# Where the Fourier groups put their second output half, and when the attention's score blocks are transposed, in a two-layer encoder kernel

## The chip, the cores and the metric

The kernel runs on one core of a Trainium2 chip. Its five instruction streams are TensorE (PE: matmuls, with its weight loads shown as PEld), VectorE (DVE), ScalarE (ACT), GpSimd (POOL) and SyncE (SP, which only issues transfers here). Each executes its own instructions in the order in which they stand in the program and waits at semaphores for the others. The metric is the device time of the core in microseconds, the median of several runs. Lower is better.

## The reference

Two encoder layers work on 272 tokens (16 learned ones ahead of 256) of width 2048, all in float32. Cut to what matters:

```python
for i in range(DEPTH):
    proj = rmsnorm(h_stream) @ w_in[i]            # q | k | v | f | gate a | gate f
    q, k = rope(rmsnorm(q, q_norm)), rope(rmsnorm(k, k_norm))
    s = einsum('bqkgd,bskd->bkgqs', q, k) / sqrt(HEAD_DIM)
    attn = einsum('bkgqs,bskd->bqkgd', softmax(s), v)           # 8 heads, 2 key/value heads
    fr = fft2(f.reshape(B, L, 8, 128), axes=(1, 3), norm="ortho").real
    merged = sigmoid(ga) * (attn @ w_attn_br[i]) + sigmoid(gf) * (fr @ w_four[i])
    h_stream += merged @ w_out[i]
    up = rmsnorm(h_stream) @ w_up[i]
    h_stream += (silu(dwconv3(up_gate)) * up_val) @ w_down[i]
return h_stream[:, N_META:]
```

## The kernel before

**Matmuls and weights.** Each operand is split into a high and a low part, and each product is three matmuls (high by high, high by low, low by high). Weights arrive as chunks of 128 x 1024 values (512 KB), in one fixed order over the whole kernel, by SP into five buffers `raw`. ACT copies each to its high part `wh` (line 303) and DVE subtracts to get the low part `wl` (line 306). There are four buffers of each, so that the splitting runs up to four chunks ahead of TensorE. A chunk of a plain group feeds 24 matmuls of 272 columns.

**Groups.** `group` (line 349 on) computes 256 output channels by 272 tokens: two chunks deep for the branch outputs `a` (attention) and the output projection `o`, four chunks for the gates `ga` and `gf`. It takes two PSUM banks. `four_group` (line 391 on) does the same for the Fourier branch `s`, in another form: its two halves m=0 and m=1 of 128 channels each take two banks (even and odd parts), are one chunk and 17 matmuls each, and are evacuated one after the other by `s_evac` (from line 1204): ACT copies `se` and `so` out (line 1207), DVE adds the other halves of the banks to them (line 1208), combines them (1210, 1211) and multiplies by the gate (1213). `s_evac` is given one buffer each of `se` and `so`, so that ACT's copy for m=1 follows DVE's line 1211 for m=0. In layer 0 the `s` chunks are first folded by DVE (line 291).

**PSUM.** There are eight banks: four under the tag "mm", which the groups take in turn, and four under "aux", which the small products take: norm statistics, score blocks `ps_s` (lines 1070 to 1072), their transposes `ps_pt` (line 1094), values `ps_pv` (lines 1117 to 1120), sums of squares `ps_ss` (line 920). The Fourier banks are also called `ps_s` in the profile; lines 409, 410 and 415 tell them apart from the scores.

**Small products between the big ones.** They are generators. After every second pair of channel tile and half (6 matmuls of a plain group, some 0.7 us) the helper `step` lets one of them go on; a `yield n` waits for n such steps. `drain` runs all of them to their end at once, with nothing between; it is called ahead of the first `a` group of a layer. So the order is that of the program text, and then a scheduler shifts instructions a little on each engine.

**Attention.** For each of the two key/value heads nine score blocks are computed: one for the learned tokens of four heads, then two blocks of 128 queries for each of four heads. A round of the loop at line 1126 issues one block's scores, takes its maximum (DVE, 1074 and 1076), its exponential with the row's sum (ACT, 1080 and 1081), two steps later the reciprocal of that sum (DVE, 1086) and the scaling of the block (POOL, 1087), and one step later the three transposes of the block *before* (PE, 1094), which ACT and DVE split into `PH` and `PL` (1107, 1108, 1110). Values of a head follow a round after its second block was transposed. Three buffers `pn` hold the exponentials. The attention of a layer starts under the `q` and `ga` groups and runs under `ga` and `gf`.

**q's norm.** `q_stage` (line 1013) gets the sums of squares of q by transposes and a reduction, makes mean plus epsilon of them (line 1030), raises that to the power -0.5 on POOL (line 515), and `attention` multiplies the result by 1/sqrt(128) (line 1049). The result scales the scores inside the exponential.

**Order of the branches.** After the `q` groups come, in the first half, `ga0 ga1 ga2 ga3 gf0 gf1 s0 gf2 a0 s1 gf3 a1 s2 ga4 a2 s3 gf4 a3`, then eight `o` groups; in the second half `s4 a4 ga5 gf5 s5 a5 ga6 gf6 s6 a6 ga7 gf7 s7 a7`, then eight `o` groups. So each layer has eight `s` groups, and each is followed at once by another group.

Of the kernel before, what the change touches and what calls it, by code (L numbers as in the profile page):

```python
# [10 lines left out]
F32 = mybir.dt.float32  # L11
# [167 lines left out]
def encoder_kernel(ctx, tc, xT, params, consts, bmat, cfold, csign, w_fl, w_f64c, w_in, w_abr, w_four, w_f64, w_out, w_up, w_down, w_vn, w_dn, w_dt, out):  # L179
# [211 lines left out]
    def four_group(key, fr, x64, w64, evac):  # L391
        k, chs = order[st["grp"]]
        assert k == key, (k, key)
        st["grp"] += 1
        i0 = st["next"]
        st["next"] += len(chs)
        advance(i0 + 1 + LOOK)
        for m in range(MG):
            sl = slice(m * P, (m + 1) * P)
            ps = [psum.tile([P, 512], F32, tag="mm", name=f"ps_s{m}{e}") for e in range(2)]  # L400
            pump(i0 + m)
            h, lo = (w.rearrange("p c n -> p (c n)").rearrange("p (e k n) -> p e k n", e=2, k=4) for w in splits.pop(i0 + m))
            for j in range(2):
                for c in range(2):
                    kt = 2 * j + c
                    for e in range(2):
                        x = al(fr[:, kt, e])
                        o2 = st2(ps[e][:, :2 * TH].rearrange("p (r n) -> p r n", r=2))
                        nc.tensor.matmul(o2, h[:, e, kt], x, start=kt == 0, stop=False)
                        nc.tensor.matmul(st2(ps[e][:, :TH]), lo[:, e, kt], x[:, 0], start=False, stop=e == 1 and kt == 3)  # L410
                    step()
                    pump()
                if m == 0 and j == 1:
                    advance(i0 + 2 + LOOK)
            nc.tensor.matmul(st2(ps[0][:, :TH]), w64[:, sl], al(x64), start=False, stop=True)
            evac(m, ps)
# [194 lines left out]
    for l in range(DEPTH):  # L611
# [6 lines left out]
        with tc.tile_pool(name=f"mix{l}", bufs=1) as mp:  # L618
# [386 lines left out]
            push(vtrans(), 4)  # L1005

            qvs, qsms, rqs = [], [], []
            pns = [mp.tile([P, 3 * P], F32, name=f"pn{i}") for i in range(3)]
            cnt = [0]
            for pn in pns:  # L1010
                nc.gpsimd.memset(pn[:, 0:P], 0.0)
# [1 line left out]
            def q_stage(i, qp, qsq, qs):  # L1013
                kv, j = i // 2, i % 2
                sl = slice(2 * j, 2 * j + 2)
                if j == 0:
                    qvs.append(small.tile([P, 9], F32, tag="qv", name="qv"))
                    qsms.append(small.tile([P, 2, 4, NM], F32, tag="sqm", name="sqm", bufs=2))
                qv, qsm = qvs[kv], qsms[kv]
                yield 3  # L1020
                nc.vector.tensor_copy(qsm[:, :, 2 * j:2 * j + 2, :], qsq[:, :, 0:NM].unsqueeze(1).to_broadcast([P, 2, 2, NM]))
                d4 = qv[:, 4 * j:4 * j + 4]
                sums_t(d4, [qsq[:, m, a:b] for m in range(MG) for a, b in BLK[1:]])
                d4 = d4.rearrange("p (m i) -> p m i", m=2)
                nc.vector.tensor_tensor(d4, d4, bc2(tok2[:, 1:3]), op=ALU.mult)
                if j:
                    yield 1
                    sums_t(qv[:, 8:9], [qsm.rearrange("p r h t -> p (r h t)")])
                    nc.vector.tensor_tensor(qv[:, 8:9], qv[:, 8:9], tok2[:, 0:1], op=ALU.mult)
                    nc.vector.tensor_scalar(qv, qv, 1.0 / HD, EPS, op0=ALU.mult, op1=ALU.add)  # L1030
                    rq = small.tile([P, 9], F32, tag="rq", name="rq")
                    pow_half(rq, qv)
                yield 6 - j
                yield from rope(qp, qs, qH[kv][:, sl, :], qL[kv][:, sl, :])
                if j:
                    rqs.append(rq)
                    if kv == 0:
                        push(attend(), 5)
# [7 lines left out]
                    yield from attention(kv, rqs[kv])  # L1046

            def attention(kv, rq):
                nc.vector.tensor_scalar(rq, rq, 1.0 / math.sqrt(HD), None, op0=ALU.mult)
                qm = mp.tile([P, 2, 2, 4, NM], F32R, tag="qm", name="qm")  # L1050
                for j, src in enumerate((qH, qL)):
                    nc.scalar.copy(qm[:, j], src[kv][:, :, 0:NM].bitcast(F32).unsqueeze(1).to_broadcast([P, 2, 4, NM]))
# [7 lines left out]
                def scores(item):  # L1060
                    if item is None:
                        lh, ll, rcol = qmh, qml, rq[:, 8:9]
                    else:
                        h, i = item
                        c0, c1 = BLK[1 + i]
                        lh, ll = qH[kv][:, h, c0:c1], qL[kv][:, h, c0:c1]
                        rcol = rq[:, 2 * h + i:2 * h + i + 1]
                    ss = psum.tile([P, 512], F32, tag="aux", name="ps_s")
                    so = st2(ss[:, :T])
                    nc.tensor.matmul(so, lh, al(kH[:, kv, :]), start=True, stop=False)  # L1070
                    nc.tensor.matmul(so, lh, al(kL[:, kv, :]), start=False, stop=False)
                    nc.tensor.matmul(so, ll, al(kH[:, kv, :]), start=False, stop=True)
                    mx = small.tile([P, 1], F32, tag="mx", name="mx")
                    nc.vector.tensor_reduce(mx, ss[:, :T], axis=AX.X, op=ALU.max)
                    nb = small.tile([P, 1], F32, tag="nb", name="nb")
                    nc.vector.tensor_scalar(nb, mx, rcol, -1.0, op0=ALU.mult, op1=ALU.mult)
                    pn = pns[cnt[0] % 3]
                    cnt[0] += 1
                    sm = small.tile([P, 1], F32, tag="sm", name="sm")
                    nc.scalar.activation(hv(pn[:, P - NM:3 * P]), de(ss[:, :T]), AF.Exp, bias=nb, scale=rcol, accum_out=sm)  # L1080
                    nc.scalar.copy(pn[:, 0:96].rearrange("p (a b) -> p a b", b=32)[:, :, 0:NM], _rep(pn[:, P - NM:P], 3))
                    return pn, sm
# [39 lines left out]
                    nc.vector.tensor_tensor(hv(qL[kv][:, h, lo:T]), de(po[:, :W]), hv(qH[kv][:, h, lo:T].bitcast(F32)), op=ALU.subtract)  # L1122

                items = [None] + [(h, i) for h in range(4) for i in range(2)]
                prev, ready, due = None, [], []
                for item in items + ["end", "end"]:
                    cur = None
                    if item != "end":
                        pe, sm = scores(item)
                    yield 2  # L1130
                    if item != "end":
                        cur = (item, normalise(pe, sm))
                    yield 1
                    if prev is not None:
                        transposed(*prev)
                        if prev[0] is not None and prev[0][1] == 1:
                            due.append(prev[0][0])
                        yield 1
                    if ready:
                        values(ready.pop(0))  # L1140
                    if prev is not None:
                        yield 1
                    ready, due = ready + due, []
                    prev = cur
                while ready:
                    values(ready.pop(0))
                    yield 1
# [425 lines left out]
```

## Time and profile before

| | |
|---|---|
| runs shown (3) | 2394.05, 2394.91, 2397.18 us; median 2394.91 |
| profiled execution | 2395.68 us, its span 2393.9 us |
| PE | 2359.2 us busy (99%), 18992 matmuls |
| DVE / ACT / POOL | 1801.8 (75%) / 1312.1 (55%) / 190.6 (8%) us busy |
| granted TensorE clock | 1.000 |
| DMA, 120 to 205 us / 357 to 467 us | 0.51 / 0.96 of the 16 engines' time |

The page gives for each engine its busy time, and for each wait the instruction that waited, the one that released it, the sum, the count and the longest. Matmuls overlap in the records: one of 272 columns is shown as 0.28 us long while the next begins 0.116 us after it. Idle time counts from the end of the last record, so a wait costs some 0.16 us more than its idle time says. In a timeline row the first number is the start, the second the duration, and the bracket at the end is the idle time ahead of the row with what ended it.

### The profile page before, as it was taken

To read this page: it belongs to the slowest core of one execution; us is meant where nothing else is said; L and a number is where in the kernel's file an instruction comes from. 1 tells how busy PE (TensorE), PEld (TensorE's weight loads), DVE (VectorE), ACT (ScalarE), POOL (GpSimd) and SP (SyncE) were. 2 spreads that over 40 slices of the span, in tenths; PEclk is the share of its full clock that TensorE was granted. 3 is DMA by queue.
4 is the path that set the end of the run, shared out by engine and by line. 5 is a ranking of instruction groups with operands and counts; after the bars stand their busy time and mean duration, and the time that the engine had idled before them with its cause. 6 is when DMAs were issued, how large, how long until landed. Compare 5 with 4: busy or idle time off the path is not lost. (4 is left out here: it accounts for less than half of the span.)

```text
span 2393.9 us, 47708 instructions
## 1 busy us (share of the span) xinstructions
PE 2359.2 (99%) x18992; PEld 2304.8 (96%) x18992; DVE 1801.8 (75%) x2817; ACT 1312.1 (55%) x1929; POOL 190.6 (8%) x301
## 2 busy tenths in 40 slices
PE   8999999999999999999999999999999999999999
PEld 8999999999999999999999999999999999999998
DVE  7787867787676556777669777766878888888798
ACT  6555544564444334445445565445677666666575
POOL 0022100100000000000000121000010000000000
PEclk9999999999999999999999999999999999999999
DMA  7556999989999999999886546888889989888887
GB/s 268 175 160 216 296 277 296 299 276 328 329 304 327 323 319 312 315 336 309 270 263 196 188 150 214 258 269 255 286 303 307 326 281 324 297 307 280 257 283 264
DMA packets 171216, 660.70 MB, mean 276 GB/s; under 512 B 19424, under 2 KB 24672, under 8 KB 170096
## 3 DMA queue, kind: packets, MB, share of 16 engines
q1 hardware_dynamic: 152528, 538.07, 64.1%
q0 software_dynamic: 17024, 117.45, 19.6%
q8 instruction: 149, 2.44, 0.4%
q10 hardware_dynamic: 1440, 2.13, 0.2%
q14 instruction: 75, 0.61, 0.1%
HBM read 635.91 MB, written 136.31 MB: 323 GB/s over the span
## 5 line engine op out<-in xcount | busy, mean ns | idle before, releaser
L306 DVE TENSOR_TENSOR wl<-raw,wh 128x1024 fp32r<-128x1024 f32 (+1 forms) x937 | 1129.2, 1217 | 474.3 <-ACT wh L303 461.2
L303 ACT CAST wh<-raw 128x1024 fp32r<-128x1024 f32 (+1 forms) x937 | 966.0, 1041 | 742.6 <-PE ps_ug L376 191.1
L375 PE MATMUL ps_ug<-xHL,wh 128*128 128x272 f32 (+1 forms) x1408 | 390.8, 278 | 0.0
L377 PE MATMUL ps_ug<-xHL,wl 128*128 128x272 f32 (+1 forms) x1408 | 390.2, 277 | 0.6 <-DVE wl L306 0.6
L376 PE MATMUL ps_ug<-xHL,wh 128*128 128x272 f32 (+1 forms) x1408 | 390.0, 277 | 0.0
L375 PEld LDWEIGHTS ps_ug<-xHL,wh 128*128 128x128 f32 x1408 | 267.4, 190 | 2.1
L376 PEld LDWEIGHTS ps_ug<-xHL,wh 128*128 128x128 f32 x1408 | 267.4, 190 | 2.1
L377 PEld LDWEIGHTS ps_ug<-xHL,wl 128*128 128x128 f32 x1408 | 267.5, 190 | 0.7 <-DVE wl L306 0.7
L375 PE MATMUL ps_uv<-xHL,wh 128*128 128x272 f32 x704 | 196.4, 279 | 0.0
L376 PE MATMUL ps_uv<-xHL,wh 128*128 128x272 f32 x704 | 196.4, 279 | 0.0
L377 PE MATMUL ps_uv<-xHL,wl 128*128 128x272 f32 x704 | 196.4, 279 | 0.0
L375 PE MATMUL ps_d<-gHL,wh 128*128 128x272 f32 x704 | 196.4, 279 | 0.0
L376 PE MATMUL ps_d<-gHL,wh 128*128 128x272 f32 x704 | 196.4, 279 | 0.0
L377 PE MATMUL ps_d<-gHL,wl 128*128 128x272 f32 x704 | 196.4, 279 | 0.0
L1416 PE MATMUL ps_p<-wh,opnd 128*128 128x512 f32 x688 | 177.1, 380 | 0.0
L560 POOL COPY tick<-wl 128x1 f32<-128x1 f32 x112 | 37.2, 332 | 1516.4 <-DVE wl L306 1516.4
L371 PE MATMUL ps_uv<-xHL,wh 128*128 128x512 f32 x448 | 149.9, 382 | 0.0
L375 PE MATMUL ps_gf<-xHL,wh 128*128 128x272 f32 (+1 forms) x512 | 143.3, 280 | 6.2 <-DVE se L1208 6.2
L375 PE MATMUL ps_ga<-xHL,wh 128*128 128x272 f32 (+1 forms) x512 | 144.1, 281 | 1.9 <-DVE se L1208 1.9
L377 PE MATMUL ps_ga<-xHL,wl 128*128 128x272 f32 (+1 forms) x512 | 141.8, 277 | 0.0
L376 PE MATMUL ps_ga<-xHL,wh 128*128 128x272 f32 (+1 forms) x512 | 141.8, 277 | 0.0
L376 PE MATMUL ps_gf<-xHL,wh 128*128 128x272 f32 (+1 forms) x512 | 141.8, 277 | 0.0
(372 smaller groups left out, 5983.7 us busy)
## 6 DMA issues: line engine op xcount, KB each, us to landing
raw<-in_w_up SPq DMA_DIRECT2D x320, 512.0 KB, 5.6
raw<-in_w_in SPq DMA_DIRECT2D x191, 512.0 KB, 4.3
raw<-in_w_down SPq DMA_DIRECT2D x88, 512.0 KB, 7.1
raw<-ft SPq DMA_DIRECT2D x80, 512.0 KB, 5.0
raw<-in_w_out SPq DMA_DIRECT2D x64, 512.0 KB, 6.0
ft<-in_w_dn POOLq DMA_DIRECT2D x30, 1024.0 KB, 12.3
raw<-in_w_dn SPq DMA_DIRECT2D x60, 512.0 KB, 5.0
raw<-in_w_abr SPq DMA_DIRECT2D x32, 512.0 KB, 4.4
```

The source lines that it names most:

```text
L303: nc.scalar.copy(h[:, a:b], r[:, a:b])
L306: nc.vector.tensor_tensor(lo[:, a:b], r[:, a:b], h[:, a:b].bitcast(F32), op=ALU.subtract)
L371: nc.tensor.matmul(o2, h[:, c, sl], ab, start=kt == 0, stop=False)
L375: nc.tensor.matmul(o, h[:, c, sl], a, start=kt == 0, stop=False)
L376: nc.tensor.matmul(o, h[:, c, sl], b, start=False, stop=False)
L377: nc.tensor.matmul(o, lo[:, c, sl], a, start=False, stop=kt == nk - 1)
L560: tc.keep_in_program_order(nc.gpsimd.tensor_copy(tick, st["wl"][:, 0, 0:1].bitcast(F32)))
L1416: nc.tensor.matmul(st2(ps[h]), x, al(w[:, 512 * h:512 * h + 512]), start=fresh and (s_, q) in BEGIN and first, stop=(s_, q) in END and end ...
```

## The change

Three edits. First, `four_group` takes the two banks of its second half (m=1) under the tag "aux" and not under "mm". Second, the attention's loop keeps up to three blocks in a list, so that the transposes (with the values that follow them) belong to the block before the last one, not to the last one; a fourth buffer `pn` is added, and one more round without scores ends the loop. Third, q's factor: the sum of squares gets 128 times epsilon added, and the power -0.5 of that holds the 1/sqrt(128), so that the multiplication at line 1049 is gone; the sums are taken two steps later (`yield 5`), and what follows them waits two steps less, so that the rotation comes where it came.

```diff
@@ four_group
-            ps = [psum.tile([P, 512], F32, tag="mm", name=f"ps_s{m}{e}") for e in range(2)]
+            ps = [psum.tile([P, 512], F32, tag="aux" if m else "mm", name=f"ps_s{m}{e}") for e in range(2)]
@@
-            pns = [mp.tile([P, 3 * P], F32, name=f"pn{i}") for i in range(3)]
+            pns = [mp.tile([P, 3 * P], F32, name=f"pn{i}") for i in range(4)]
@@ q_stage
-                yield 3
+                yield 5
...
-                    nc.vector.tensor_scalar(qv, qv, 1.0 / HD, EPS, op0=ALU.mult, op1=ALU.add)
+                    nc.vector.tensor_scalar(qv, qv, HD * EPS, None, op0=ALU.add)
                     rq = small.tile([P, 9], F32, tag="rq", name="rq")
                     pow_half(rq, qv)
-                yield 6 - j
+                yield 4 - j
@@ attention
-                nc.vector.tensor_scalar(rq, rq, 1.0 / math.sqrt(HD), None, op0=ALU.mult)
...
-                    pn = pns[cnt[0] % 3]
+                    pn = pns[cnt[0] % 4]
...
-                prev, ready, due = None, [], []
-                for item in items + ["end", "end"]:
-                    cur = None
+                lag, ready, due = [], [], []
+                for item in items + ["end"] * 3:
                     if item != "end":
                         pe, sm = scores(item)
                     yield 2
                     if item != "end":
-                        cur = (item, normalise(pe, sm))
+                        lag.append((item, normalise(pe, sm)))
                     yield 1
-                    if prev is not None:
-                        transposed(*prev)
-                        if prev[0] is not None and prev[0][1] == 1:
-                            due.append(prev[0][0])
+                    done = lag.pop(0) if len(lag) == 3 or lag and item == "end" else None
+                    if done is not None:
+                        transposed(*done)
+                        if done[0] is not None and done[0][1] == 1:
+                            due.append(done[0][0])
                         yield 1
                     if ready:
                         values(ready.pop(0))
-                    if prev is not None:
+                    if done is not None:
                         yield 1
                     ready, due = ready + due, []
-                    prev = cur
```

The number of matmuls is the same. The rows that follow are from the order of the instructions, before and with the change; line numbers after the second edit are one or two lower with the change.

On PE at the beginning of layer 0's attention the small products stood so before (the rows between them are matmuls of the groups `q3` and `ga0`, left out):

```order
L1070 MATMUL ps_s_1719<-kH_828,qm_1675 128x272
...
L1070 MATMUL ps_s_1765<-kH_828,q1_1382 128x272
...
L1094 MATMUL ps_pt_1799<-cst_72,pn0_1223 128x128 x3
...
L1070 MATMUL ps_s_1825<-kH_828,q1_1382 128x272
...
L1094 MATMUL ps_pt_1867<-cst_72,pn1_1224 128x128 x3
```

And with the change:

```order
L1069 MATMUL ps_s_1720<-kH_828,qm_1676 128x272
...
L1069 MATMUL ps_s_1758<-kH_828,q1_1384 128x272
...
L1069 MATMUL ps_s_1800<-kH_828,q1_1384 128x272
...
L1093 MATMUL ps_pt_1836<-cst_72,pn0_1223 128x128 x3
...
L1069 MATMUL ps_s_1864<-kH_828,q1_1384 128x272
...
L1093 MATMUL ps_pt_1915<-cst_72,pn1_1224 128x128 x3
```

The first block (`pn0`) is transposed after the scores of the third block and no longer after those of the second; each later one moves by one block too. 18 group matmuls stand between one block's scores and the next until the first transposes; from there on a round has 30.

On PE in layer 1 the end of the attention stood so before, around the Fourier group s0 (`ps_s00`, `ps_s10`), the gate group gf2 and the group a0:

```order
L1094 MATMUL ps_pt_18648<-cst_72,pn1_16189 128x128 x3
L409 MATMUL ps_s00_18662<-fr_15848,wh496_18514 128x276
...
L1117 MATMUL ps_pv_18668<-PH_18118,VH_15859 128x258
...
L1094 MATMUL ps_pt_18713<-cst_72,pn2_16190 128x128 x3
...
L415 MATMUL ps_s10_18707<-x64_15849,w64_18242 128x138
...
L1117 MATMUL ps_pv_18772<-PH_18118,VH_15859 128x258
...
L375 MATMUL ps_1_a_0_0_18891<-q1_16382,wh502_18802 128x258
```

And with the change:

```order
L409 MATMUL ps_s00_18648<-fr_15848,wh496_18504 128x276
...
L1093 MATMUL ps_pt_18654<-cst_72,pn3_16191 128x128 x3
...
L1093 MATMUL ps_pt_18704<-cst_72,pn0_16188 128x128 x3
...
L1116 MATMUL ps_pv_18715<-PH_18142,VH_15859 128x258
...
L415 MATMUL ps_s10_18690<-x64_15849,w64_18232 128x138
...
L1093 MATMUL ps_pt_18771<-cst_72,pn1_16189 128x128 x3
...
L1116 MATMUL ps_pv_18814<-PH_18142,VH_15859 128x258
...
L375 MATMUL ps_1_a_0_0_18891<-q1_16384,wh502_18792 128x258
```

One more set of transposes now stands in s0 and one in gf2, and the last values have moved from 12 matmuls into gf2 to 48 of its 96; they still stand ahead of a0. In layer 0 the last values, which stood 24 matmuls ahead of s0, now stand in s0's first half.

On DVE at layer 0's s0 the order was (chunks 64 and 65 are those of s0, 66 to 69 those of gf2):

```order
L306 TENSOR_TENSOR wl66_3087<-raw66_2828,wh66_3086 128x1024
L1122 TENSOR_TENSOR q2_1383<-ps_pv_3068,q1_1382 128x272
L1185 TENSOR_TENSOR th_3111<-ps_0_gf_1_0_2943,rstdB_80 128x272
L1185 TENSOR_TENSOR th_3111<-ps_0_gf_1_1_2944,rstdB_80 128x272
L306 TENSOR_TENSOR wl67_3125<-raw67_2882,wh67_3124 128x1024
L306 TENSOR_TENSOR wl68_3160<-raw68_2945,wh68_3159 128x1024
L1208 TENSOR_TENSOR se_3143<-ps_s00_3118,se_3143 128x138
```

And with the change:

```order
L306 TENSOR_TENSOR wl66_3077<-raw66_2814,wh66_3076 128x1024
L1107 TENSOR_TENSOR PL_2442<-ps_pt_3069,PH_2441 128x2x128
L1109 TENSOR_TENSOR PH_2441<-ps_pt_3069,PH_2441 16x128
L1183 TENSOR_TENSOR th_3101<-ps_0_gf_1_0_2936,rstdB_80 128x272
L1183 TENSOR_TENSOR th_3101<-ps_0_gf_1_1_2937,rstdB_80 128x272
L306 TENSOR_TENSOR wl67_3115<-raw67_2862,wh67_3114 128x1024
L1121 TENSOR_TENSOR q2_1385<-ps_pv_3122,q1_1384 128x272
L306 TENSOR_TENSOR wl68_3160<-raw68_2938,wh68_3159 128x1024
L1206 TENSOR_TENSOR se_3143<-ps_s00_3108,se_3143 128x138
```

The splitting of a transposed block has come ahead of gf1's evacuation, and the splitting of a value product between the chunks 67 and 68. At the later `s` groups (s1 to s7 of both layers) the order on DVE is the same as before.

## The prediction

> **What bounds the kernel now.** I read the page's span and first part first, then the waits of PE, then the timeline around the longest ones.
>
> ```profile
> span 2393.9 us, 47708 instructions
> PE 2359.2 (99%) x18992; PEld 2304.8 (96%) x18992; DVE 1801.8 (75%) x2817; ACT 1312.1 (55%) x1929; POOL 190.6 (8%) x301
> ```
>
> PE is busy 99% of the span, so nothing but PE's own waits can be won: 2393.9 - 2359.2 = 34.7 us of idle time, and a little more, because a wait also breaks the overlap of matmuls. The number of matmuls does not change. What of the idle time can the three edits reach? The waits of PE, in the form engine, what was issued, for whom it waited, sum in us, times, longest:
>
> ```profile
> PE ps_a L375 <- DVE se L1208: 6.5, 8, 1.9
> PE ps_gf L375 <- DVE se L1208: 6.2, 6, 2.0
> ...
> PE ps_pt L1094 <- POOL pn L1087: 5.1, 5, 1.4
> PE ps_ga L375 <- DVE se L1208: 1.9, 2, 1.3
> PE ps_pv L1117 <- ACT PH L1107: 1.6, 3, 0.6
> PE ps_pv L1118 <- DVE PL L1108: 1.2, 1, 1.2
> PE ps_ss L920 <- ACT qps L912: 1.0, 2, 0.8
> ```
>
> 8 + 6 + 2 = 16 waits on `se`, one behind each Fourier group, 6.5 + 6.2 + 1.9 = 14.6 us idle: the first edit's. Five waits of transposes on POOL, 5.1 us: the second's. Two of the sums of squares, 1.0 us: the third's. The values' waits (1.6 + 1.2) lie behind the transposes and are to be watched. One engine, one sum: what these waits lose, the span loses, unless something else is late right behind them.
>
> **First edit: the banks.** The longest wait stands behind layer 0's s0. PE first, then DVE and ACT around it:
>
> ```profile
> 227.38 0.27 PE L415 MATMUL ps_s<-x,w 96*128 96x138 f32 x1
> 229.69 0.38 PE L375 MATMUL ps_gf<-xHL,wh 128*128 128x272 f32 x1 [2.03 <-DVE se L1208]
> ```
>
> ```profile
> 223.27 1.22 DVE L306 TENSOR_TENSOR wl<-raw,wh 128x1024 fp32r<-128x1024 f32 x1
> 224.88 0.78 DVE L1185 TENSOR_TENSOR th<-ps_gf,rstdB 128x272 f32<-128x272 f32 x2
> 226.83 2.58 DVE L306 TENSOR_TENSOR wl<-raw,wh 128x1024 fp32r<-128x1024 f32 x2 [1.18 <-ACT wh L303]
> 229.34 0.29 DVE L1208 TENSOR_TENSOR se<-ps_s,se 128x138 f32<-128x138 f32 x1
> 229.55 0.29 DVE L1208 TENSOR_TENSOR so<-ps_s,so 128x138 f32<-128x138 f32 x1
> ```
>
> ```profile
> 228.07 0.27 ACT L1207 COPY se<-ps_s 128x138 f32<-128x138 f32 x1
> ```
>
> gf2 takes the banks of s0's first half. They are free when DVE has added `se`; ACT had copied by 228.34, but DVE was in two chunk splittings (226.83 to 229.41) that stand ahead in its order. With the edit the four "mm" banks go: two to gf1, two to s0's first half, two to gf2. gf2 now gets gf1's banks, which DVE emptied (line 1185) by 224.88 + 0.78 = 225.66, while s0 ends at 227.65. That leaves 2.0 us. The order of DVE shows 0.42 + 0.28 us of `PL` and `PH` moved in ahead of line 1185 at this place; some 1.2 us of margin stay. At s1 the group before is a0:
>
> ```profile
> 247.93 0.43 DVE L1227 SCALAR_TENSOR_TENSOR th<-th,ps_a 128x272 f32<-128x272 f32 x1
> ...
> 250.21 0.27 PE L415 MATMUL ps_s<-x,w 96*128 96x138 f32 x1
> 252.08 0.38 PE L375 MATMUL ps_gf<-xHL,wh 128*128 128x272 f32 x1 [1.59 <-DVE se L1208]
> ```
>
> Emptied by 248.36 against 250.48: 2.1 us of margin with nothing moved in.
>
> What is the next thing that could be late? The next group's chunks: `wl` of gf2's first chunk is done at 223.27 + 1.22 = 224.49, of its second and third by 229.41, used about 3 and 6 us into gf2 (24 matmuls at 0.116 us are 2.8 us each), that is at 230.5 and 233.3 even if gf2 begins at 227.45. So PE does not fall upon a missing weight. DVE's lateness remains where it is, and is covered by PE working on gf2. The second half's "aux" banks are wanted next by whoever takes aux banks: after s0 of either layer the attention's last blocks, at s1 to s7 nobody.
>
> Size: 227.38 to 229.69 is 2.31 us from start to start where 0.07 to 0.12 is the pace of matmuls, so the wait costs 2.2 us and not 2.03. The same at the short waits of layer 1:
>
> ```profile
> 1516.83 0.27 PE L415 MATMUL ps_s<-x,w 96*128 96x138 f32 x1
> 1517.66 0.38 PE L375 MATMUL ps_gf<-xHL,wh 128*128 128x258 f32 x1 [0.56 <-DVE se L1208]
> ```
>
> 0.83 - 0.09 = 0.74 for an idle time of 0.56: 0.18 more. The sum is 14.6 + 16 x 0.18 = **17.5 us** (bounds 14.6, the idle time alone, and 17.9, with a pace of 0.07). All of it lies on PE.
>
> **Second edit: transposes a block later.** The beginning of layer 0's attention, first PE's score matmul, DVE and POOL, then PE:
>
> ```profile
> 173.95 0.28 PE L1070 MATMUL ps_s<-kH,qm 128*128 128x272 f32 x1
> ...
> 178.00 1.23 DVE L306 TENSOR_TENSOR wl<-raw,wh 128x1024 fp32r<-128x1024 f32 x1 [0.18 <-ACT wh L303]
> 178.25 3.30 POOL L1087 TENSOR_SCALAR pn<-pn,rs 128x384 f32<-128x384 f32 x2 [11.38 <-ACT pn L1081]
> ...
> 178.59 0.28 PE L376 MATMUL ps_ga<-xHL,wh 128*128 128x272 f32 x1
> 178.70 0.28 PE L377 MATMUL ps_ga<-xHL,wl 128*128 128x272 f32 x1
> 180.39 0.55 PE L1094 MATMUL ps_pt<-cst,pn 128*128 128x128 f32 x3 [1.41 <-POOL pn L1087]
> ```
>
> ```profile
> L1087 POOL TENSOR_SCALAR pn<-pn,rs x36: 1234/1246/2137, 128.0 to 1450.1; 128x384 f32<-128x384 f32 x36
> ```
>
> The chain from the first score to its transposes takes 180.39 - 173.95 = 6.44 us; PE came to the transposes after 178.70 + 0.11 - 173.95 = 4.9 us. With the edit 18 more group matmuls and a further score block come in between, 18 x 0.116 = 2.1 and some 0.35: about 7.3 us against 6.44, a margin of 0.9. Later blocks gain a whole round of 30 matmuls, 3.5 us, against waits of at most 1.4. So all five waits should go; a residue at the four starts of a key/value head is possible, 0.2 us each. Gain: 5.1 + 5 x 0.18 = 6.0, less 0.8: **5.2 us** (bounds 0 and 6.0). The fourth buffer keeps the exponential of the next block from waiting for the later transposes.
>
> [...] The first of the two scalings took 3.30 - 1.24 = 2.06 us where the median is 1.246, and DVE was in a chunk splitting from 178.00 to 179.23. [...]
>
> Where does the stall go? The values' matmuls wait for `PH` and `PL`, which follow the transposes at the same distance in the order as before, a round of 30 matmuls for the first of the pair and no more for the second. I take their waits (2.8 us idle, all shown) as unchanged; with the transposes no longer late they might lessen, up to 2.8 + 4 x 0.18 = 3.5 us won, or, since PE comes earlier to the values by what the transposes no longer wait, they might spread (a rival below). At layer 1's s0 the attention's last transposes and values now share the aux banks with s0's second half, and the order shows values that take a bank of transposes issued a little ahead: a stall of 0.5 to 1 us once is likely. I take **-0.7 us** (bounds 0 and -2).
>
> **Third edit.** The multiplication at line 1049 goes: four DVE instructions on 9 columns, off PE's path, worth nothing beside DVE's 75%. The sums of squares come two steps, 12 matmuls or 1.4 us, later behind ACT's copy `qps`; their two waits of at most 0.8 go: 1.0 + 2 x 0.18 = 1.36, taken as **1.2 us** (bounds 0 and 1.4). What follows waits two steps less, so the rotation comes where it came; the factor reaches the first scores' exponential 1.4 us later, which the later transposes cover.
>
> **Sum.** 17.5 + 5.2 - 0.7 + 1.2 = 23.2 us, off the profiled execution's 2395.68 (span 2393.9 and 1.8 around it), which lies 0.8 above the median of the runs, 2394.91. Off the median: **2371.7 us**, 1.0% less.
>
> **Rivals.**
>
> *The attention gives back its part.* PE reaches the values earlier, and `PH`/`PL` are made by ACT and DVE between other work. For it: four values wait already, up to 1.2. Against it: 12 of 16 don't, and the distance in PE's order is the same. If the other 12 waited 0.88 each (2.8 / 4 + 0.18), 10.6 us: 2371.7 + 10.6 = 2382.3. With the first edit's gain alone it is 2394.9 - 17.5 + 0.7 = 2378.1, so this case is 2377 to 2383.
>
> *Transfers cannot follow.* Three stretches (length, then busy time of PE, PEld, DVE, ACT and POOL, granted clock, DMA share, GB/s):
>
> ```profile
> 120.00:205.00 85.00, 81.99 (x706) 81.27 (x706) 64.40 (x141) 51.14 (x116) 27.13 (x19) 1.00 0.51 163
> 357.00:467.00 110.00, 105.67 (x908) 105.11 (x907) 80.94 (x130) 52.48 (x78) 10.63 (x22) 1.00 0.96 302
> 1360.00:1455.00 95.00, 89.86 (x782) 88.03 (x781) 69.57 (x156) 58.44 (x130) 28.11 (x19) 1.00 0.48 152
> ```
>
> In the second, the DMA engines are busy for 0.96. Four Fourier groups lie there, with some 5.2 us to win. If 0.97 is the ceiling, the stretch needs 110 x 0.96 / 0.97 = 108.9 us and only 1.1 us can be won: 4.1 lost, 2375.8. Against it: five raw and four split buffers ahead, which a gap of 5 us in 110 need not empty. The clock is 1.00 throughout, so no throttling gives a gain back.
>
> *Slower.* One mechanism: the attention's chain through DVE. In the order DVE now has more of a block's work between a score and its reciprocal. Waits of all engines show the chain to be tight:
>
> ```profile
> DVE rs L1086 <- ACT pn L1080: 11.1, 15, 1.1
> ...
> ACT pn L1080 <- DVE nb L1076: 20.3, 14, 2.3
> ```
>
> DVE stands still up to 1.1 and ACT up to 2.3 us in one block. If a block held DVE for x more, its free time in the two attention stretches would go first, 85 - 64.4 = 20.6 and 95 - 69.6 = 25.4, over 18 blocks each (36 rows of L1087); what exceeds it comes late on PE through the chunk splittings. With the first edit's gain and the rest kept, the total gets slower than 2394.9 only from 36x = 46 + 23.2, x = 1.9 us, and beyond the measurable from 2.05. At x = 2.3 the loss is 36 x 2.3 - 46 = 36.8: 2371.7 + 36.8 = 2408.5. Against it: the order moves no wait of DVE's ahead of a splitting except at one place.
>
> *It doesn't do what it says.* The aux banks of the second half of s0 to s7 are awaited in the place of the mm banks, or DVE's lateness reappears one group later, and the time stays at about 2394. For it: DVE does no less work. Against it: at s1 to s7 nobody else takes aux banks, and DVE has the next 2.8 us and more of a chunk to catch up 2 us.
>
> **How the numbers follow.** Forecast 0.68 (own range 2367 to 2376, from 28 us won, if the values' waits lessen too, to 19, with the first edit at its idle time and 1 us lost besides); attention gives back 0.17; transfers 0.06; no effect 0.04; slower 0.05. The range of 8 in 10 goes from 2367, the forecast's best, to 2383, which takes in the first two rivals. What three runs can tell from no change is about 0.2%, 4.8 us: faster 0.68 + 0.17 + 0.06 - 0.01 = 0.90, same 0.05, slower 0.05.
>
> **What would show it.** Right: among PE's waits no line with `se`; the row of gf2 behind s0 starts 0.1 us after the last Fourier matmul; `ps_pt` on POOL below 1 us; `ps_ss` gone; `ps_pv` still about 3 us; PE's busy time unchanged and its idle time near 13. Wrong: `ps_gf` or `ps_a` on DVE's line 1183 or 1225 (the earlier group's banks late too), `ps_s` waiting at line 409 for an aux bank, `ps_pv` at 10 us or more, or new waits on `wl` in 205 to 467, where a `wl` behind `raw` would mean the transfers.

## The result, and the profile after

| | before | changed |
|---|---|---|
| median of the runs (4 each) | 2394.48 us (2392.85 to 2397.18) | 2377.97 us (2377.10 to 2378.34) |
| ratio | | 0.9929, 95% interval 0.9912 to 0.9947 |
| profiled execution's span | 2393.9 us | 2375.2 us |

The change makes the kernel 0.7% faster: 16.5 us by the medians, 18.7 us between the two profiled executions. Forecast was 2371.7 us, 23.2 us less; the time lies inside the range of 2367 to 2383, 2 us outside the forecast's own range (2367 to 2376), and about 6 us above the forecast. The question behind the prediction is therefore: which of the three edits gave less than its term, and where did those microseconds go?

The page's first rows of the changed kernel, and then all of PE's waits above 0.5 us:

```profile
span 2375.2 us, 47690 instructions
PE 2357.5 (99%) x18992; PEld 2305.7 (97%) x18992; DVE 1802.9 (76%) x2813; ACT 1313.3 (55%) x1929; POOL 191.5 (8%) x303
```

```profile
PE ps_f L442 <- ACT wh L303: 5.1, 2, 4.5
PE ps_f L845 <- DVE qp L913: 2.6, 1, 2.6
PE ps_pv L1116 <- ACT PH L1106: 2.3, 4, 1.0
PE ps_pv L1117 <- DVE PL L1107: 2.0, 4, 1.1
PE ps_o L376 <- DVE mL L1228: 1.4, 1, 1.4
PE ps_ug L377 <- DVE wl L306: 0.6, 2, 0.4
```

All 16 waits on `se` are gone, those of the transposes on POOL and of `ps_ss` too. New or longer are three: `ps_f` on `qp` (0.9 before), the values `ps_pv` (2.8 before), and `ps_o` on `mL` (none before). `ps_f` on `wh` stands at the program's start and no edit touches it.

What the steps did, place by place, can be had from start to start: the time between two matmuls' starts less the usual pace at that place (0.11 us behind a Fourier group), from the two profiled executions.

| place | before, us | changed, us | difference | forecast |
|---|---|---|---|---|
| Fourier group to the next group (16) | 17.2 | 0 | -17.2 | -17.5 |
| transposes on `pn` | 6.15 | 0.14 | -6.0 | -5.2 |
| sums of squares on `qps` | 1.34 | 0 | -1.3 | -1.2 |
| values on `PH`/`PL` | 3.4 | 6.1 | +2.7 | 0, and 0.7 for shared banks |
| `ps_f` on `qp`, layer 1 | 1.06 | 2.78 | +1.7 | 0 |
| slow matmuls right behind that wait | 0 | 1.65 | +1.65 | 0 |
| `o0` on `mL`, layer 0 | 0 | 1.58 | +1.6 | 0 |

The sum is -16.9 of the 18.7 between the spans. Of the rest, 0.9 us stands at the program's start, where `ps_f` waited 5.1 us for `wh` and not 6.0; what is left is small pieces. So each of the three removed waits gave what it was to give, and three tenths of the 24.5 us came back in four places.

The first edit at the place with the longest wait (s0 of layer 0), PE and then DVE:

```profile
223.49 0.27 PE L415 MATMUL ps_s<-x,w 96*128 96x138 f32 x1
223.60 0.33 PE L375 MATMUL ps_gf<-xHL,wh 128*128 128x272 f32 x1
```

```profile
220.16 0.79 DVE L1183 TENSOR_TENSOR th<-ps_gf,rstdB 128x272 f32<-128x272 f32 x2
...
223.96 0.29 DVE L1206 TENSOR_TENSOR se<-ps_s,se 128x138 f32<-128x138 f32 x1
```

gf2 begins 0.11 us after the Fourier group's last matmul, where it began 2.31 us after it. DVE adds `se` 0.47 us after that last matmul's start (1.96 us before, with two splittings ahead of it), and nobody waits for it now. The banks that gf2 takes were emptied at 220.95, 2.65 us before gf2 began.

The second edit at the beginning of layer 0's second key/value head, PE:

```profile
173.77 0.28 PE L1069 MATMUL ps_s<-kH,qm 128*128 128x272 f32 x1
...
181.06 0.49 PE L1093 MATMUL ps_pt<-cst,pn 128*128 128x128 f32 x3
```

From the first score to its transposes there are 7.29 us now, worked out beforehand as 7.3, and no wait in the row.

### The profile page after: what moved, and what is told of

Its sections match the earlier page's. It is cut to its first block, busy times and chain, and to the rows that moved or that the text cites. A ratio compares the mean times of both kernels' runs of the same rounds, so it can differ in the third digit from the quotient of the medians.

```text
span 2375.2 us, 47690 instructions
## 1 busy us (share of the span) xinstructions
PE 2357.5 (99%) x18992; PEld 2305.7 (97%) x18992; DVE 1802.9 (76%) x2813; ACT 1313.3 (55%) x1929; POOL 191.5 (8%) x303
## 5 line engine op out<-in xcount | busy, mean ns | idle before, releaser
L375 PE MATMUL ps_ga<-xHL,wh 128*128 128x272 f32 (+1 forms) x512 | 143.9, 281 | 0.0
L376 PE MATMUL ps_o<-mL,wh 128*128 128x272 f32 (+1 forms) x512 | 141.9, 277 | 1.4 <-DVE mL L1228 1.4
L377 PE MATMUL ps_gf<-xHL,wl 128*128 128x272 f32 (+1 forms) x512 | 141.8, 277 | 0.0
```

The source lines that it names most:

```text
L375: nc.tensor.matmul(o, h[:, c, sl], a, start=kt == 0, stop=False)
L376: nc.tensor.matmul(o, h[:, c, sl], b, start=False, stop=False)
L377: nc.tensor.matmul(o, lo[:, c, sl], a, start=False, stop=kt == nk - 1)
```

## The experiments

All were timed against the kernel before on the same chip. "Start to start" is as in the table above.

### Each edit alone

**Banks.** Only this line of the kernel before was changed:

```diff
-            ps = [psum.tile([P, 512], F32, tag="mm", name=f"ps_s{m}{e}") for e in range(2)]
+            ps = [psum.tile([P, 512], F32, tag="aux" if m else "mm", name=f"ps_s{m}{e}") for e in range(2)]
```

> The kernel before with the first edit alone (second Fourier half into the aux banks). Ledger theory (each wait of the changed kernel belongs to the edit at whose place it stands): the 16 waits on se go (18.0 us from start to start), and a wait of o0 on mL at the end of layer 0's branches appears (about 1.5 us); the waits of the transposes (5 us) and of ps_ss (1 us) stay: 16.5 us less than before, ratio 0.9931. Rival: the wait on mL and the values' longer waits come with the transposes' move and not with the banks; then 18 us less, ratio 0.9925, and no wait on mL.

Measured: 2378.37 us, ratio 0.9932 (0.9919 to 0.9946), 17.3 us less. No wait on `se` is left, and the other waits of the kernel before stand there unchanged:

```profile
PE ps_pt L1094 <- POOL pn L1087: 5.1, 5, 1.4
...
PE ps_pv L1117 <- ACT PH L1107: 1.6, 3, 0.6
PE ps_pv L1118 <- DVE PL L1108: 1.2, 1, 1.2
PE ps_ss L920 <- ACT qps L912: 1.0, 2, 0.8
PE ps_f L845 <- DVE qp L913: 0.9, 1, 0.9
...
PE ps_o L376 <- DVE mL L1230: 0.3, 1, 0.3
```

This one line is worth as much as the whole change: beside it the other two edits gave nothing that the intervals tell apart (0.9932 against 0.9929, and 0.9921 when the change was measured again). The wait on `mL` exists here too, but with 0.3 us and not 1.4.

**Lag.** The loop with the list and the fourth `pn`, nothing else:

```diff
-            pns = [mp.tile([P, 3 * P], F32, name=f"pn{i}") for i in range(3)]
+            pns = [mp.tile([P, 3 * P], F32, name=f"pn{i}") for i in range(4)]
...
-                prev, ready, due = None, [], []
+                lag, ready, due = [], [], []
...
```

> The kernel before with the second edit alone (transposes a block later, fourth pn buffer). Ledger theory: the waits on POOL's pn go (6.1 us), the values' waits grow from 3.4 to about 6 us, waits on se stay at 14 to 15 us: 3.5 us less than before, ratio 0.9985. Rival, the prediction's: the values' waits stay at 3, 5.2 us less or more, ratio 0.9978 or lower. Second rival: the values' growth in the changed kernel comes from q's edit; then they stay at 3 here too.

Measured: 2388.12 us, ratio 0.9969 (0.9957 to 0.9980), 7.5 us less. That is twice the ledger's 3.5 and more than the prediction's 5.2; the interval excludes the ledger's ratio. Its waits:

```profile
PE ps_a L375 <- DVE se L1207: 5.5, 8, 1.0
...
PE ps_gf L375 <- DVE se L1207: 4.2, 5, 1.3
PE ps_pv L1117 <- ACT PH L1107: 2.8, 3, 1.7
PE ps_ga L375 <- DVE se L1207: 1.9, 2, 1.3
PE ps_pv L1118 <- DVE PL L1108: 1.5, 3, 1.1
```

The transposes' waits are gone, the values' grew from 2.8 to 4.3 us (so the growth does come with the later transposes), and the waits on `se` fell by 3.0 us: mostly at the two s0, where the order on DVE is another, and at one place near 390 us, where the execution before had waited 0.9 us longer. The parts overlap: what is won at the s0 here is won by the banks anyway.

**q.** Factor and later sums, on the kernel before:

```diff
-                yield 3
+                yield 5
...
-                    nc.vector.tensor_scalar(qv, qv, 1.0 / HD, EPS, op0=ALU.mult, op1=ALU.add)
+                    nc.vector.tensor_scalar(qv, qv, HD * EPS, None, op0=ALU.add)
...
-                yield 6 - j
+                yield 4 - j
...
-                nc.vector.tensor_scalar(rq, rq, 1.0 / math.sqrt(HD), None, op0=ALU.mult)
```

> The kernel before with the third edit alone (q's factor under the power, sums two steps later). Ledger theory: PE's waits on ps_ss go (1.3 us), but in layer 1 PE then comes earlier to a group that waits for DVE's evacuation of q, that wait grows from 0.9 to about 2.6 us, and behind it the granted clock falls to about 0.6 for 4 us (1.6 us lost): 2 us more than before, ratio 1.0008. The prediction's: 1.2 us less, ratio 0.9995, and no such stretch of slow clock.

Measured: 2394.49 us, ratio 0.9997 (0.9989 to 1.0006). The time is the prediction's (0.9995) rather than the ledger's (1.0008), which lies just outside the interval. But the trace shows what the ledger expected, a wait on `qp` of 2.4 us and a mean clock of 0.63 over 4 us behind it; so something else in this edit gives back as much. The next runs take the edit apart.

```profile
PE ps_f L845 <- DVE qp L913: 2.4, 1, 2.4
```

### q's edit taken apart

**The change with the sums at their old step** (`no_yield5`).

```diff
-                yield 5
+                yield 3
...
-                yield 4 - j
+                yield 6 - j
```

> The changed kernel with q's sums at their old step (the factor stays under the power). Ledger theory: two waits on ps_ss come back (1.0 us idle), the wait of ps_f on qp falls from 2.6 to about 0.9 us, and there is no stretch of granted clock 0.6 near 1285 us: 2.0 us less than the changed kernel, about 2376. The prediction's: 1.2 us more than the changed kernel, about 2379.

Measured: 2371.68 us (2371.21 to 2372.82), ratio 0.9901 (0.9887 to 0.9914). It was to be 2 us better than the changed kernel; it is 4.8 better by the ratio of the changed kernel's second measurement below (0.9921), and 6.3 by the medians with the first. Its waits:

```profile
PE ps_pv L1117 <- DVE PL L1107: 1.5, 3, 1.1
PE ps_pv L1116 <- ACT PH L1106: 1.3, 3, 0.6
PE ps_ss L920 <- ACT qps L912: 1.0, 2, 0.8
PE ps_f L845 <- DVE qp L913: 0.9, 1, 0.9
...
PE ps_o L376 <- DVE mL L1228: 0.3, 1, 0.3
```

The wait on `ps_ss` is back (1.34 us start to start), but that on `qp` is down by 1.7, the slow matmuls (1.65) are gone, and so are 2.2 us of the values' waits in layer 1, which I had put to the transposes. The two DVE stretches show a difference in order there. With the sums at the old step:

```profile
1344.51 0.72 DVE L930 TENSOR_TENSOR qs<-qs,cst 128x544 f32<-128x544 f32 x1
...
1347.20 0.43 DVE L1073 TENSOR_REDUCE mx<-ps_s 128x1 f32<-128x272 f32 x1
```

and in the changed kernel:

```profile
1350.79 0.43 DVE L1073 TENSOR_REDUCE mx<-ps_s 128x1 f32<-128x272 f32 x1
...
1351.66 0.44 DVE L1073 TENSOR_REDUCE mx<-ps_s 128x1 f32<-128x272 f32 x1 [0.19 <-PE ps_s L1071]
...
1352.31 0.73 DVE L930 TENSOR_TENSOR qs<-qs,cst 128x544 f32<-128x544 f32 x1
```

A rotation of q (L930 and what follows it) stands ahead of the first score block's maximum in the one and behind the second's in the other, so it falls into the attention's chain. That this order is the cause of the 2.2 us is read from the traces; that they belong to the later sums is shown.

**One step later instead of two** (`yield_4`).

```diff
-                yield 5
+                yield 4
...
-                yield 4 - j
+                yield 5 - j
```

> The changed kernel with q's sums one step later than before and not two. Theory (a PE wait of up to about 2.2 us leaves the granted clock at 1.00, one of 2.5 us or more brings it to about 0.6 for 4 us): the wait of ps_f on qp comes out between 0.9 and 2.0 us, a rest of about 0.5 us stays at ps_ss, the clock behind stays at 1.00, and the 1.6 us of slow matmuls are gone. If the values' waits in layer 1 fall too, as with the sums at their old step, the time is near 2372 (ratio 0.990); if they stay, 2374.5 (0.991). Rival (the slow clock belongs to something else than the length of that wait): the clock is at 0.6 there again, 2376.

Measured: 2376.33 us, ratio 0.9922 (0.9908 to 0.9935), the rival's time. The wait on `qp` is 1.6 us (1.72 start to start), 0.5 us stays at `ps_ss`, as expected, and 0.6 us of the transposes' waits is back; but the clock falls again (a mean of 0.59 over 4.2 us), and the values' waits stay (3.7 us idle). My theory that the length of the wait decides on the clock has fallen with this run; more on it in the last section.

```profile
PE ps_f L845 <- DVE qp L913: 1.6, 1, 1.6
PE ps_pt L1093 <- POOL pn L1086: 0.6, 1, 0.6
```

**The factor alone** (`only_fold`), on the kernel before:

```diff
-                    nc.vector.tensor_scalar(qv, qv, 1.0 / HD, EPS, op0=ALU.mult, op1=ALU.add)
+                    nc.vector.tensor_scalar(qv, qv, HD * EPS, None, op0=ALU.add)
...
-                nc.vector.tensor_scalar(rq, rq, 1.0 / math.sqrt(HD), None, op0=ALU.mult)
```

> The kernel before with q's factor under the power alone: sums at their old step, transposes and banks as before. The prediction's step: four multiplications of 0.17 us gone, off PE's path, 0 us. Theory: the multiplication makes DVE stand for POOL's power, 7.4 us in four waits, with splits and score work queued behind it; without it the waits of transposes and values in layer 1 (2.7 and 3.4 us from start to start) fall together by 1 to 2 us, ratio 0.9992 to 0.9996.

Measured: 2392.61 us, ratio 0.9989 (0.9980 to 0.9998), 2.3 us less. The prediction's step, nothing, lies outside the interval. The transposes' wait on `pn`, 5.1 us before, is 2.9 here; the values' waits are as before.

```profile
PE ps_pt L1093 <- POOL pn L1086: 2.9, 3, 1.5
```

**Banks and lag without q's edit** (`banks_and_lag`), so the kernel of no_yield5 with the multiplication back.

> The kernel before with the first and second edits, without the third: no_yield5 without the factor under the power, so with the multiplication back. The prediction's step (the multiplication off PE's path, worth nothing): 2371.7 like no_yield5, within 0.7 us. Rival, from the run with the second edit alone, where one value's wait at the start of the second key/value head was 1.8 us and not 0.4: the multiplication delays that start in layer 1, 1.5 us more, 2373.2.

Measured: 2373.86 us, ratio 0.9912 (0.9898 to 0.9925), 2.6 us above no_yield5 by the ratios, where the prediction's step said nothing and the rival 1.5. The two profiled executions are 1.1 us apart, and the values' waits 1.5 (4.3 us idle against 2.8). The intervals overlap, but only_fold says the same with its own. DVE, at the beginning of layer 1's second head:

```profile
1352.93 0.17 DVE L1030 TENSOR_SCALAR qv<-qv 128x9 f32<-128x9 f32 x1
1355.37 0.17 DVE L1049 TENSOR_SCALAR rq<-rq 128x9 f32<-128x9 f32 x1 [2.27 <-POOL rq L515]
1355.45 1.22 DVE L306 TENSOR_TENSOR wl<-raw,wh 128x1024 fp32r<-128x1024 f32 x1
```

The multiplication itself takes 0.17 us, but DVE stands 2.27 us ahead of it until POOL's power is done, with a chunk splitting, a reciprocal and a transposed block's low parts queued behind it. In the kernel before the row for this wait was in the trace, and I had not weighed it:

```profile
DVE rq L1049 <- POOL rq L515: 7.4, 4, 1.9
```

### What the values wait for

The kernel of no_yield5 with the values of a head ahead of the round's transposes (`values_first`):

```diff
+                    if ready:
+                        values(ready.pop(0))
                     if done is not None:
+                        yield 1
                         transposed(*done)
...
                         yield 1
-                    if ready:
-                        values(ready.pop(0))
-                    if done is not None:
-                        yield 1
```

> The kernel of no_yield5 with the values of a head issued ahead of the round's transposes and no longer one step behind them. Theory: the values wait for the high and low parts of the transposes issued directly ahead of them, which belong to another block and which they don't need; then their waits (2.8 us idle, 3.9 from start to start) fall below 0.7 us and the time by about 3.3 us against no_yield5, to 2368.4. Rival: they wait because ACT and DVE are behind in general; then the wait stays at 2 us or more or stands at the transposes (ps_pt on an aux bank or on pn) and the time stays at 2371 to 2372.

Measured: 2370.58 us (2370.22 to 2371.45), ratio 0.9898 (0.9885 to 0.9912), the fastest of all runs, though not told apart from no_yield5 (0.9901).

```profile
PE ps_pv L1117 <- DVE PL L1107: 1.8, 2, 1.1
PE ps_o L376 <- DVE mL L1227: 1.5, 1, 1.5
```

From start to start, three of the six values' waits are gone (0.37, 0.34 and 0.76 us), as the theory has it: they were for a block that these values don't use. Of the last values of layer 1's attention, in the rounds without scores, 1.6 of 2.0 us stay, and the last wait in layer 0 grew from 0.44 to 1.26: 2.8 us in all against 3.9, a drop of 1.1 (1.6 with every small gap among the values' matmuls counted) and not of 3.3. The theory holds for the rounds with scores; in the short rounds at the end the values come close behind their own block. This execution also had 1.3 us more at `mL`, which the next part explains.

### The wait on mL

The changed kernel once more:

> The changed kernel once more, beside the others of this call. Whether o0's wait on mL (1.4 us idle) at the end of layer 0's branches belongs to the kernel or to one execution's transfers: if to the kernel, 1.4 us again; if to transfers, 0.3 us as in the run without the later sums, and the wait on qp (2.6 us) with its slow clock and the values' waits (4.3 us) stay. Time 2377 to 2379 in either case.

Measured: 2376.29 us, ratio 0.9921 (0.9907 to 0.9934). The wait on `mL` is 0.8 us here, between the two expectations. Its neighbours explain it. PE at the beginning of o0 in the first profile of the change, and ACT ahead of it:

```profile
454.63 0.28 PE L375 MATMUL ps_o<-mH,wh 128*128 128x272 f32 x1
456.33 0.38 PE L376 MATMUL ps_o<-mL,wh 128*128 128x272 f32 x1 [1.42 <-DVE mL L1228]
```

```profile
445.19 1.04 ACT L303 CAST wh<-raw 128x1024 fp32r<-128x1024 f32 x1 [1.04 <-DMA raw<-in_w_out]
```

From 446.3 on DVE has no gap until `mL` is written, so every delay ahead of that reaches PE. Over the profiles of kernels with the banks' edit, ACT's last wait for a transfer in this stretch against PE's wait on `mL`, start to start:

| kernel | ACT's wait for raw, after 430 us | PE's wait on `mL` |
|---|---|---|
| no_yield5 | 0 | 0.44 |
| banks_and_lag | 0 | 0.43 |
| only_banks | 0 | 0.44 |
| yield_4 | 0 | 0.44 |
| changed, second profile | 0.44 | 0.98 |
| changed, first profile | 1.04 | 1.58 |
| half_loads (below) | 1.06 | 1.61 |
| values_first | 1.38 | 1.75 |

0.44 us belong to the kernel: with the gap behind s7 gone, DVE is that much late at the end of the branches. The rest is the transfer's lateness of that execution, passed on nearly one to one. In half_loads the late chunk is one of `in_w_in` (six such waits in layer 0's branches, 12.2 us, and none for `in_w_out`); in the three others that show one it is a chunk of the output projection.

Is it the amount of data? The changed kernel with less of it (`half_loads`). It leaves out the second half of eight Fourier chunks and folds the first half with itself, so it computes other products:

```diff
-        nc.sync.dma_start(r, src)
+        if i in folded and i >= 110:
+            nc.sync.dma_start(r[:, 0:2], src[:, 0:2])
+        else:
+            nc.sync.dma_start(r, src)
```

> The changed kernel with only half of each of the eight Fourier chunks s4 to s7 of layer 0 loaded (2 MB less of some 34 MB in the last 110 us of its branches; the other half is replaced by the loaded one, so these products are not the reference's). If transfers hold the end of layer 0's branches: ACT's waits for raw between 205 and 455 us fall from 10 us to below 3, o0's wait on mL falls from 1.4 to 0.3 us, and the time by about 1 us against the changed kernel of this call. If DVE's own lateness holds it: 1.4 us of wait and the time unchanged.

Measured: 2377.12 us, ratio 0.9922 (0.9910 to 0.9934), unchanged. The DMA share between 341 and 451 us falls from 0.98 to 0.94, but ACT's waits for raw in layer 0's branches stay (12 us), and the wait on `mL` is 1.4 us. So taking these bytes away did not take the late transfers away. What makes single transfers late by a microsecond in some executions stays open.

## Why the prediction was right or wrong

- **Banks: right.** 17.5 us forecast, 17.2 in the trace at the 16 places, 17.3 us by the medians with this edit alone. The margins held everywhere: the next group's banks were empty, its weights split. The 0.18 us that a wait costs beyond its idle time was a little high (17.2 - 14.6 = 2.6 us over 16 waits, 0.16 each).
- **The stall for shared banks (-0.7 us): wrong, it did not come.** At layer 1's s0 nothing waits for an aux bank; the values' wait there is for `PL`.
- **Transposes: right.** 5.2 forecast, 6.0 measured at the transposes. The residue at the four starts was 0.14 us in all. That held although in layer 1 a pair of scalings took 4.79 us (up to 2.33 each, where the median is 1.245), with rotations (0.70 to 1.03 us an instruction) and two chunk splittings (1.2 us each) running on DVE.

```profile
1353.60 4.79 POOL L1086 TENSOR_SCALAR pn<-pn,rs 128x384 f32<-128x384 f32 x2 [21.07 <-ACT pn L1080]
```

- **"I take their waits as unchanged" (the values): mis-sized by 2.7 us.** The rival that the attention gives back its part was to cost 10.6 us; it cost a quarter of that. That the time came out in this rival's band (2377 to 2383) is chance: most of what came back did so elsewhere. Of the 2.7 us, 2.2 belong to q's later sums and half a microsecond is left for the transposes beside the factor; without the factor the later transposes alone cost 1.5 us of idle time there.
- **"Worth nothing beside DVE's 75%" (the multiplication): wrong, by 2.3 to 2.6 us in the kernel's favour.** The busy share of 75% does not show that DVE stood still for the multiplication with other work queued behind it; the row of 7.4 us stood in the trace of before.
- **"Their two waits go ... taken as 1.2 us" (the later sums): the step that failed, 1.3 us gained and 5.5 lost.** The wait went, and PE came 1.34 us earlier to a group that is bound by DVE's evacuation of q: the wait there grew by 1.7. Behind it the matmuls ran slow (1.65 us, at a mean clock of 0.58 over 4 us), where the forecast had the clock at 1.00 throughout, and the rotation on DVE fell behind score blocks (2.2). "What follows waits two steps less, so the rotation comes where it came" holds for the step count, not for DVE's order. By the runs, the later sums cost 4.8 to 6.3 us net (in the first profile 1.1 us of the difference is the late transfer), nearly all of what separates 2371.7 from 2376 to 2378; without them the time is 2371.68. That it meets the forecast is partly luck: the factor's gain, which I had at zero, stands there for the 1.2 us of the sums, which this kernel does not win, for the 0.44 us at `mL` and for smaller misses.
- **Transfers cannot follow: a part.** I had 4.1 us for a ceiling of 0.97 on the DMA share, an assumption of mine that no run shows: from 341 to 451 us the changed kernel had 0.98, with PE busy for 110.00 of 110 us. But single late transfers cost 0 to 1.3 us at the end of layer 0's branches, where no gap hides them any more.
- **Slower: no.** With sums at the old step DVE's chain had the slack; with the later sums it was this kind of mechanism, in one place, that by the traces took 2.2 us of the loss, and DVE's evacuation of q another 1.7.

## What to carry to other kernels

Before a wait is taken away, look at the next place at which the same engine meets the late one: if a second engine is the bound in between, as DVE is between two evacuations of q, the wait may only move, and to a worse place: here 1.34 us went at `ps_ss`, and 1.72 us came at `qp`, with 1.65 us of slow matmuls behind. A tiny instruction is not free where its engine stands still for it with other work queued behind, as here, where DVE stood 2.27 us for one of 0.17 us; look it up among the waits of its engine, not by its duration. And when several edits are made in one change, take them apart: here one line gave 17.3 us, the second edit and the factor together some 6.7 more, and a shift by two steps took 5 or 6 back.

## What the hardware showed that was not expected

In the profiles of all four kernels with the sums two steps later or one step later (the changed kernel has two), TensorE's granted clock was low over the 4 us or so behind the wait on `qp`: a mean of 0.63 in only_q, 0.71 in the changed kernel's second profile, 0.59 in yield_4, 0.50 in half_loads. In the changed kernel's first profile it was 0.50 for 3.41 us, from 1286.05 to 1289.46, which begins 0.9 us after the wait's end. The windows below are not drawn to that stretch, so they show a mean of 0.58 or 0.59 over some 4 us. The changed kernel, the kernel before at the same place, the kernel before behind s0, and the kernel with the sums one step later (window, length, busy time of PE, PEld, DVE, ACT and POOL, clock, DMA share, GB/s):

```profile
1285.40:1289.40 4.00, 4.00 (x22) 3.82 (x22) 3.60 (x7) 1.99 (x2) 0.00 (x0) 0.58 0.70 207
```

```profile
1299.40:1303.40 4.00, 4.00 (x35) 3.85 (x36) 3.60 (x6) 1.99 (x2) 0.00 (x0) 1.00 0.67 201
229.60:233.60 4.00, 3.92 (x33) 3.92 (x34) 3.84 (x12) 1.65 (x4) 0.00 (x0) 1.00 1.00 193
```

```profile
1283.50:1287.70 4.20, 4.18 (x21) 4.00 (x22) 3.78 (x6) 1.99 (x2) 0.00 (x0) 0.59 0.63 191
```

22 matmuls are done in 4 us where 35 are done otherwise; PE's busy share shows nothing of it, since the matmuls are shown as longer (0.54 us for one of 276 columns, where it is 0.33 us at the same place before). PE had stood 2.6 us in the first, 0.9 in the second, 2.0 in the third and 1.6 in the fourth. So 1.6 us of idle time had the low clock behind them at this place, and 2.0 us at s0 had not: the length alone does not decide.

Nor does the place. Such a stretch takes 0.0007 off the mean clock of an execution (0.50 x 3.41 of 2375 us, an estimate from the changed kernel's trace), and two of the five executions of yield_4 have a mean of 1.000, which leaves no room for it: they took 2373.8 and 2374.2 us, the other three 2376.3 to 2378.0. Of the changed kernel's second five, one has 1.000, and it is the fastest. In 24 of 40 executions of the kernel before that were timed beside the experiments the mean is below 1.000, with no trace kept that says where. What decides is not shown.
